# Masked softmax of a matrix product on one core: rows gathered over four batches in 16 KB runs, and the mask read as whole half-blocks

## The chip, the core and the metric

The kernel runs on one core of a Trainium2 chip. The metric is device time in microseconds. The core has a matrix engine (PE, TensorE), a vector engine (DVE), an activation engine (ACT), GpSimd (POOL), a queue engine that issues transfers (SP), and 16 DMA engines that move data between the chip's HBM and the on-chip memory SBUF. Products land in PSUM banks and are read from there by DVE and ACT. A transfer of 128 partitions is cut into one packet for each contiguous run and spread over the 16 DMA engines.

## What is computed

```
y = scale * matmul(x, weight)          # x: 16 x 512 x 512, weight: 512 x 512, scale 0.125
y = where(mask == 1, y, -1e9)          # mask: 1 below the diagonal, 0 on it and above
out = softmax(y, axis=-1)              # float32, 16 x 512 x 512
```

The mask is strictly lower triangular: row r sees the columns below r. Rows 0 to 255 (the upper half, h=0) thus need only the first 256 columns of the product, rows 256 to 511 (the lower half, h=1) all 512. Row 0 sees nothing, so its result is uniform, 1/512.

## The kernel before

The work is cut into 16 units. Unit u takes the half h = u % 2 of two neighbouring batches: 512 rows, put on 128 partitions with four neighbouring rows (8 KB) in each. Each unit is one load of 1 MB (`load`, L80), one tile of four row slots, and one store of 1 MB (`store`, L160). Eight input tiles and eight output tiles exist, so unit u+8 uses the tile of unit u.

A unit goes through these steps, each a function:

- `cast` (L85, DVE): x to bf16, one instruction of 128x2048.
- `transpose` (L94, PE): 16 products with the identity, four row slots by four pieces of the inner dimension, into two PSUM tiles.
- `evict` (L104 on DVE, L105 on ACT): one PSUM tile each to SBUF.
- `multiply`: per row slot four matmuls over the inner dimension (L118) with 256 or 512 columns, one matmul (L127) that adds the band of the mask (identity by `band`, 256 columns), and on ACT the exponential with its row sum (L137).
- `normalise`: a reciprocal (L152) and four scalings (L154) on DVE; in upper units POOL writes 1/512 over row 0 (L156).

The mask enters as an additive band: 0 where the mask is 1 and -512 where it is 0. Only the 128x128 blocks on the diagonal are read (256 KB, L164, runs of 512 B). DVE turns them into `diag_bf`, four matmuls with a 0/1 matrix `spread` (L208) put each row where its unit's layout has it, and eight copies (L215, four on DVE and four on ACT) write them into `band`. The rest of `band` is constant and set by memsets.

The order on every engine is the program's order. The opening issues the loads of x for unit 0, of the mask, of the weight and of units 1 to 7 in one row on SP. PE warms up with 12 products of zeros (L173). After the opening, the loop over u does `transpose(u+1)`, `cast(u+2)`, `evict(u+1)`, `multiply(u)`, `normalise(u-1)`, `store(u-1)`, and the load of unit u+7:

```python
        if u >= 1:
            normalise(u - 1)
            store(u - 1)
            if u - 1 + X_BUFS < U:
                load(u - 1 + X_BUFS)
```

SP therefore issues stores and loads one behind another: a load waits on SP until the store ahead of it may be issued. On DVE, `cast(u+2)` stands before `evict(u+1)`: when x of unit u+2 hasn't landed, the eviction waits behind it.

The softmax here doesn't subtract the row's maximum and nothing guards it: scores larger than these inputs give would overflow.

## Time and profile before

| | before |
|---|---|
| time, median of 8 runs | 90.92 us (90.84 to 91.13) |
| time of the profiled execution | 91.02 us |
| its span, first to last instruction | 89.2 us |
| mean granted PE clock | 0.944 |
| busy: PE, DVE, ACT, POOL | 69.7, 60.5, 55.3, 7.3 us |
| DMA: moved, packets, share of 16 engines' span | 34.87 MB, 5280, 93.6% |
| x of one unit (1 MB), issue to landing, median | 14.6 us |
| store of one unit (1 MB), issue to landing, median | 11.6 us |
| weight (1 MB) and mask (256 KB), issue to landing | 8.5 and 6.6 us |

The time is what the device reports for a run; the span is what the profile sees of one execution, 1.8 us less. Busy shares are averages over the span; which engine is the limit must be read stage by stage. An issue-to-landing time holds the waiting behind transfers issued earlier, so it says how far ahead of the DMA engines the queue is, not how long the transfer itself takes. A packet count rests on the length of contiguous runs: 8 KB for x, the output and the weight, 512 B for the mask, and a few bytes for the count-up at the end of each engine's share of a transfer.

### The profile page before, as it was taken

The page shows a single profiled execution, that of the slowest core. Times are in us where ns is not written, and L with a number is a line of the kernel's source. Part 1 is how long each engine was busy: PE and PEld are TensorE (multiplying, and loading weights), DVE is VectorE, ACT ScalarE, POOL GpSimd, SP SyncE. Part 2 cuts the span into 40 slices and gives each one's busy share as a digit, 9 for nine tenths or more (in the row PEclk, how much of TensorE's full clock was granted, in tenths as well). Part 3 has the DMA queues.
Part 4 walks back from the last instruction along what each step waited for, and adds up shares of the span by engine and source line. Part 5 has one row for each costly group of instructions (what it writes and reads, how often), then busy time and mean ns, then how long its engine had stood idle before and what let it go on. Part 6 is the DMA issues. An engine that isn't in the chain of part 4 may idle for free.

```text
span 89.2 us, 1610 instructions
## 1 busy us (share of the span) xinstructions
PE 69.7 (78%) x584; PEld 48.7 (55%) x592; DVE 60.5 (68%) x123; ACT 55.3 (62%) x154; POOL 7.3 (8%) x20
## 2 busy tenths in 40 slices
PE   4946205999999999999999999999999999900000
PEld 1305005794697589569748956975895595400000
DVE  5876914779299949959994996987494996262000
ACT  5402930668787778778777977877797787630000
POOL 7620000002000200200020020002000201000000
PEclk9999997599999999999999999999999999999555
DMA  0869999999999999999999999999999999999960
GB/s 0 323 216 365 419 422 430 437 415 422 419 430 419 419 433 433 404 419 426 433 415 433 437 404 426 433 430 415 426 422 430 415 433 433 419 422 441 426 294 29
DMA packets 5286, 34.95 MB, mean 392 GB/s; under 512 B 544, under 2 KB 1056, under 8 KB 1056
## 3 DMA queue, kind: packets, MB, share of 16 engines
q1 hardware_dynamic: 5280, 34.87, 93.6%
q8 instruction: 4, 0.07, 0.3%
q14 instruction: 2, 0.02, 0.0%
HBM read 18.09 MB, written 16.78 MB: 391 GB/s over the span
## 4 chain that ended last, share of the span: by engine, by line
PE 71%; DMA 12%; DVE 3%; SPq 2%; issue 1%; ACT 1%; DVEq 0%; ACTq 0%
PE py L118 47%; PE pt L94 16%; DMA xf<-in_x_dram 12%; PE py L127 8%; DVE ot L154 1%; DVE xb L85 1%; SPq L80 1%; ACT ot L137 1%; SPq L164 1%; SPq L165 1%; DVEq L264 0%; DVE rinv L152 0%; ACTq L264 0%
## 5 line engine op out<-in xcount | busy, mean ns | idle before, releaser
L118 PE MATMUL py<-w_bf,xt 128*128 128x256 bf16 (+1 forms) x248 | 49.8, 328 | 0.4
L137 ACT ACTIVATE ot<-py 128x256 f32<-128x256 f32 (+1 forms) x64 | 31.2, 493 | 7.7 <-PE py L127 7.4
L118 PEld LDWEIGHTS <-xt 128*128 128x128 bf16 x256 | 24.8, 100 | 12.2
L105 ACT COPY xt<-pt 128x1024 bf16<-128x1024 bf16 x16 | 16.2, 1012 | 14.9 <-PE pt L94 10.3
L85 DVE CAST xb<-xf 128x2048 bf16<-128x2048 f32 x16 | 19.5, 1222 | 7.7 <-DMA xf<-in_x_dram 7.5
L154 DVE TENSOR_SCALAR ot<-ot,rinv 128x256 f32<-128x256 f32 (+1 forms) x64 | 23.5, 431 | 0.8
L94 PE MATMUL pt<-ident_bf,xb 128*128 128x128 bf16 x256 | 17.8, 225 | 6.6 <-DVE xb L85 6.6
L94 PEld LDWEIGHTS <-xb 128*128 128x128 bf16 x256 | 16.6, 116 | 8.5 <-DVE xb L85 7.6
L127 PE MATMUL py<-band,ident_bf 128*128 128x256 bf16 x64 | 17.6, 275 | 0.0
L104 DVE COPY xt<-pt 128x1024 bf16<-128x1024 bf16 x16 | 11.0, 686 | 6.2 <-PE pt L94 6.2
L137 ACT ACTIVATION_READ_ACCUMULATOR ot<-py 128x1 f32 x64 | 12.8, 200 | 0.0
L156 POOL MEMSET ot<- 2x256 f32 x8 | 3.6, 450 | 66.5 <-DVE ot L154 66.5
L127 PEld LDWEIGHTS <-ident_bf 128*128 128x128 bf16 x64 | 6.3, 99 | 4.2
L173 PE MATMUL py<-zeros 128*128 128x512 bf16 x12 | 4.2, 518 | 1.2 <-DVE zeros L170 1.2
L152 DVE RECIPROCAL rinv<-rsum 128x4 f32<-128x4 f32 x16 | 2.7, 168 | 3.2 <-ACT ot L137 3.2
L179 DVE MEMSET ot<- 128x1024 f32 x4 | 3.6, 912 | 0.6 <-issue 0.6
L173 PEld LDWEIGHTS <-zeros 128*128 128x128 bf16 x12 | 1.4, 124 | 3.5 <-issue 1.9
L186 ACT ACT_TABLE_LOAD x1 | 1.3, 1283 | 0.7 <-PEq L250 0.7
L215 ACT CAST band<-py 64x256 bf16<-64x256 f32 x4 | 1.4, 368 | 0.1
L215 DVE CAST band<-py 64x256 bf16<-64x256 f32 x4 | 1.4, 406 | 0.0
L180 POOL MEMSET ot<- 2x256 f32 x4 | 1.2, 301 | 1.5 <-DVE ot L179 1.4
L208 PE MATMUL py<-diag_bf,spread 128*128 128x512 bf16 x4 | 1.0, 377 | 0.2 <-DVE diag_bf L194 0.2
(14 smaller groups left out, 6.6 us busy)
## 6 DMA issues: line engine op xcount, KB each, us to landing
xf<-in_x_dram SPq DMA_DIRECT2D x16, 1024.0 KB, 14.6
out_dram<-ot SPq DMA_DIRECT2D x16, 1024.0 KB, 11.6
w_f<-in_weight_dram SPq DMA_DIRECT2D x1, 1024.0 KB, 8.5
diag_f<-in_mask_dram SPq DMA_DIRECT2D x1, 256.0 KB, 6.6
```

The source lines that it names most:

```text
L85: seq(nc.vector.tensor_copy(xb, st_x.pop(u)))
L94: nc.tensor.transpose(st_pt[u][kt // 2][:, kt % 2, t], xb[:, t].rearrange("p (k kt) -> p kt k", kt=KT)[:, kt], ident_bf,)
L104: seq(nc.vector.tensor_copy(xt[:, 0:2], pt[0]))
L105: seq(nc.scalar.copy(xt[:, 2:4], pt[1]))
L118: nc.tensor.matmul(py[:, :NC], lhsT=xt[:, kt, t], rhs=w_bf[:, kt, :NC], start=(kt == 0), stop=(kt == KT - 1),)
L127: nc.tensor.matmul(py[:, h * HB : NC], lhsT=ident_bf, rhs=band[:, h, t], start=False, stop=True, skip_group_check=True,)
L137: nc.scalar.activation(out=ot[:, t, :NC], in_=py[:, :NC], func=AF.Exp, bias=0.0, scale=float(scale), accum_out=rsum[:, t : t + 1],)
L154: seq(nc.vector.tensor_scalar_mul(ot[:, t, :NC], ot[:, t, :NC], rinv[:, t : t + 1]))
L156: seq(nc.gpsimd.memset(ot[0:2, 0, :HB], 1.0 / N))
L173: seq(nc.tensor.matmul(idle, lhsT=zeros[:, :P], rhs=zeros, start=True, stop=True))
L179: nc.vector.memset(ots[i][:, :, HB:], 0.0)
L215: seq(copy(band[half, :, t, g * P : (g + 1) * P], src[half, :, g]))
```

## The change

Units stay at 512 rows, but two of them now form a group that is loaded and stored together. A group takes one half h of four neighbouring batches: 32 blocks of eight neighbouring rows from each, so a partition holds eight rows, a run of 16 KB. Unit u is row slots 0 to 3 or 4 to 7 of group u // 2 (`slots`), so the halves come in the order upper, upper, lower, lower. `load` and `store` move 2 MB; only the first group is loaded in two pieces of 1 MB, and the first and the last group are stored in two pieces. There are five input tiles and four output tiles of 2 MB.

The mask: partition q now gets rows 2q and 2q+1 of each half as one run of 3 KB (768 numbers, from which the 256 columns of each row's band are taken), 786 KB in all, in two half-blocks. Two DVE instructions make `band` from it. The placing of rows moves into the product that adds the band: `spread[:, j]`, a 0/1 matrix, stands in the place of the identity as the stationary operand (L127 of before). The four placing products, the eight copies, the memsets of `band` and `diag_bf` go away. The mask lands in the last output tile, which is used late.

The opening loads x of unit 0, the weight, the mask, x of unit 1, and then groups 1 to 4. A second run of 12 products of zeros stands after `transpose(0)`. In the first two turns of the loop `multiply(u)` stands ahead of `transpose(u+1)`. The pools of `xb` and `xt` have two tiles each, where they had three.

```diff
-X_BUFS = 8
-OUT_BUFS = 8
-WARM = 12
+X_BUFS = 5
+OUT_BUFS = 4
...
-    xb_pool = ctx.enter_context(tc.tile_pool(name="xb", bufs=3))
-    xt_pool = ctx.enter_context(tc.tile_pool(name="xt", bufs=3))
+    xb_pool = ctx.enter_context(tc.tile_pool(name="xb", bufs=2))
+    xt_pool = ctx.enter_context(tc.tile_pool(name="xt", bufs=2))
...
-    x_r = x.rearrange("(c e) (h p t) k -> c h p e (t k)", e=2, h=2, t=T)
-    out_r = out.rearrange("(c e) (h p t) n -> c h p e (t n)", e=2, h=2, t=T)
-
-    diag_r = bass.AP(tensor=mask.tensor, offset=mask.offset, ap=[[N, P], [P * N + P, KT], [1, P]])
-
+    x_r = x.rearrange("(c e) (h p t) k -> c h p e (t k)", e=E, h=2, t=S)
+    out_r = out.rearrange("(c e) (h p t) n -> c h p e (t n)", e=E, h=2, t=S)
     ident_bf = const.tile([P, P], BF16, name="ident_bf")
     w_f32 = const.tile([P, KT, N], FP32, name="w_f32")
     w_bf = const.tile([P, KT, N], BF16, name="w_bf")
-    diag_f32 = const.tile([P, KT, P], FP32, name="diag_f32")
-    diag_bf = const.tile([P, KT, P], BF16, name="diag_bf")
-    spread = const.tile([P, T, P], BF16, name="spread")
+    spread = const.tile([P, S // 2, P], BF16, name="spread")
     zeros = const.tile([P, N], BF16, name="zeros")
-    band = const.tile([P, 2, T, HB], BF16, name="band")
-    ots = [const.tile([P, T, N], FP32, name=f"ot{i}") for i in range(OUT_BUFS)]
+    band = const.tile([P, 2, 2, HB], BF16, name="band")
+    ots = [const.tile([P, S, N], FP32, name=f"ot{i}") for i in range(OUT_BUFS)]
...
-    def load(u):
-        xf = x_pool.tile([P, T, K], FP32, name="xf")
-        seq(nc.sync.dma_start(xf.rearrange("p t k -> p (t k)"), x_r[u // 2, u % 2]))
-        st_x[u] = xf
+    def slots(u):
+        return slice(T * (u % 2), T * (u % 2) + T)
+
+    def load(g, part=slice(0, S)):
+        if g not in st_x:
+            st_x[g] = x_pool.tile([P, S, K], FP32, name="xf")
+        run = slice(part.start * K, part.stop * K)
+        seq(nc.sync.dma_start(st_x[g].rearrange("p t k -> p (t k)")[:, run], x_r[g // 2, g % 2][:, :, run]))
 
     def cast(u):
         xb = xb_pool.tile([P, T, K], BF16, name="xb")
-        seq(nc.vector.tensor_copy(xb, st_x.pop(u)))
+        seq(nc.vector.tensor_copy(xb, st_x[u // 2][:, slots(u)]))
...
-        h = u % 2
+        h = u // 2 % 2
         NC = (h + 1) * HB
         xt = st_xt.pop(u)
-        ot = ots[u % OUT_BUFS]
+        ot = ots[u // 2 % OUT_BUFS][:, slots(u)]
...
-                    lhsT=ident_bf,
-                    rhs=band[:, h, t],
+                    lhsT=spread[:, (slots(u).start + t) // 2],
+                    rhs=band[:, h, t % 2],
...
-        if u % 2 == 0:
-            seq(nc.gpsimd.memset(ot[0:2, 0, :HB], 1.0 / N))
-
-    def store(u):
-        ot = ots[u % OUT_BUFS]
-        seq(nc.sync.dma_start(out_r[u // 2, u % 2], ot.rearrange("p t n -> p (t n)")))
-
-
-    load(0)
-    seq(nc.sync.dma_start(diag_f32, diag_r))
+        if u % 4 == 0:
+            seq(nc.gpsimd.memset(ot[0:E, 0, :HB], 1.0 / N))
+
+    def store(g, part=slice(0, S)):
+        ot = ots[g % OUT_BUFS]
+        run = slice(part.start * N, part.stop * N)
+        seq(nc.sync.dma_start(out_r[g // 2, g % 2][:, :, run], ot.rearrange("p t n -> p (t n)")[:, run]))
+
+
+    load(0, slots(0))
     seq(nc.sync.dma_start(w_f32, weight.rearrange("(p kt) n -> p kt n", kt=KT)))
-    for u in range(1, X_BUFS):
-        load(u)
+
+
+    RUN = N + HB
+    mask_f32 = ots[OUT_BUFS - 1].rearrange("p t n -> p (t n)")[:, : 2 * RUN].rearrange(
+        "p (h c) -> p h c", h=2
+    )
+    seq(
+        nc.sync.dma_start(
+            mask_f32,
+            bass.AP(
+                tensor=mask.tensor,
+                offset=mask.offset,
+                ap=[[2 * N, P], [HB * (N + 1), 2], [1, RUN]],
+            ),
+        )
+    )
+    load(0, slots(1))
+    for g in range(1, X_BUFS):
+        load(g)
 
 
     nc.vector.memset(zeros, 0.0)
-    idle = psum_y.tile([P, N], FP32, name="py")
-    for _ in range(WARM):
-        seq(nc.tensor.matmul(idle, lhsT=zeros[:, :P], rhs=zeros, start=True, stop=True))
+
+    def spin(n):
+        idle = psum_y.tile([P, N], FP32, name="py")
+        for _ in range(n):
+            seq(nc.tensor.matmul(idle, lhsT=zeros[:, :P], rhs=zeros, start=True, stop=True))
+
+    spin(12)
 
     make_identity(nc, ident_bf)
-    nc.gpsimd.memset(band[:HP, :, :, P:], MASK_NEG)
-    nc.gpsimd.memset(band[HP:, :, :, :P], 0.0)
     for i in range(0, OUT_BUFS, 2):
         nc.vector.memset(ots[i][:, :, HB:], 0.0)
-        nc.gpsimd.memset(ots[i][0:2, 0, HB:], 1.0 / N)
-
-
-    for g in range(2):
-        for e in range(2):
-            seq(
-                nc.scalar.copy(
-                    spread.rearrange("k t (g p e) -> k t g p e", g=2, e=2)[:, :, g, :, e],
-                    ident_bf.rearrange("k (p t) -> k t p", t=T),
-                )
-            )
+        nc.gpsimd.memset(ots[i][0:E, 0, HB:], 1.0 / N)
+
+
+    for e in range(E):
+        seq(
+            nc.scalar.copy(
+                spread.rearrange("q j (p e) -> q j p e", e=E)[:, :, :, e],
+                ident_bf.rearrange("q (p j) -> q j p", j=S // 2),
+            )
...
     cast(0)
-    seq(
-        nc.vector.tensor_scalar(
-            out=diag_bf,
-            in0=diag_f32,
-            scalar1=-MASK_NEG,
-            scalar2=MASK_NEG,
-            op0=ALU.mult,
-            op1=ALU.add,
-        )
-    )
     transpose(0)
+    spin(12)
     evict(0)
-    for t in range(T):
-        pm = psum_y.tile([P, N], FP32, name="py")
-        seq(
-            nc.tensor.matmul(
-                pm, lhsT=spread[:, t], rhs=diag_bf.rearrange("k b c -> k (b c)"), start=True, stop=True
-            )
-        )
-        for g, copy in enumerate((nc.vector.tensor_copy, nc.scalar.copy)):
-            half = slice(g * HP, (g + 1) * HP)
-            src = pm.rearrange("p (h g c) -> p h g c", h=2, g=2)
-            seq(copy(band[half, :, t, g * P : (g + 1) * P], src[half, :, g]))
     seq(nc.vector.tensor_copy(w_bf[:, 0:2], w_f32[:, 0:2]))
     seq(nc.scalar.copy(w_bf[:, 2:4], w_f32[:, 2:4]))
+    for i in range(2):
+        seq(
+            nc.vector.tensor_scalar(
+                out=band[:, :, i],
+                in0=mask_f32[:, :, i * N : i * N + HB],
+                scalar1=-MASK_NEG,
+                scalar2=MASK_NEG,
+                op0=ALU.mult,
+                op1=ALU.add,
+            )
+        )
     cast(1)
 
+
     for u in range(U + 1):
+        if u < 2:
+            multiply(u)
         if u + 1 < U:
             transpose(u + 1)
         if u + 2 < U:
             cast(u + 2)
         if u + 1 < U:
             evict(u + 1)
-        if u < U:
+        if 2 <= u < U:
             multiply(u)
         if u >= 1:
             normalise(u - 1)
-            store(u - 1)
-            if u - 1 + X_BUFS < U:
-                load(u - 1 + X_BUFS)
+            g, second = divmod(u - 1, 2)
+            if g in (0, G - 1):
+                store(g, slots(u - 1))
+            elif second:
+                store(g)
+            if second and g + X_BUFS < G:
+                load(g + X_BUFS)
```

## The prediction

> **What bounds the kernel now.** I read the page's slices first, then the queue, then the chain of waits, then windows of the DMA's rate, and last the timeline at both ends.
>
> ```profile
> PE   4946205999999999999999999999999999900000
> ...
> DMA  0869999999999999999999999999999999999960
> ...
> DMA packets 5286, 34.95 MB, mean 392 GB/s; under 512 B 544, under 2 KB 1056, under 8 KB 1056
> ...
> q1 hardware_dynamic: 5280, 34.87, 93.6%
> ...
> PE 71%; DMA 12%; DVE 3%; SPq 2%; issue 1%; ACT 1%; DVEq 0%; ACTq 0%
> ```
>
> The chain gives PE 71%, but it follows instructions. The slices show TensorE falling silent after slice 34 while the transfers go on for three more. So I ask how long the DMA engines were ever short of work (columns: stretch, its length, busy of PE, PEld, DVE, ACT, POOL, clock, DMA share, GB/s):
>
> ```profile
> 2.00:5.00 3.00, 3.00 (x11) 1.12 (x9) 2.51 (x4) 0.98 (x5) 1.95 (x5) 1.00 0.85 317
> 5.00:7.50 2.50, 0.61 (x6) 0.24 (x5) 1.66 (x2) 0.00 (x0) 0.30 (x1) 1.00 0.51 164
> 7.50:22.00 14.50, 9.47 (x82) 7.08 (x81) 9.57 (x18) 7.99 (x18) 0.45 (x1) 0.88 1.02 428
> 22.00:57.00 35.00, 34.79 (x319) 25.42 (x321) 28.73 (x60) 27.73 (x79) 1.79 (x4) 1.00 1.01 423
> 57.00:86.00 29.00, 20.98 (x175) 14.51 (x176) 17.02 (x41) 17.32 (x53) 1.35 (x3) 0.94 1.01 426
> 86.00:88.30 2.30, 0.00 (x0) 0.00 (x0) 0.00 (x0) 0.00 (x0) 0.00 (x0) 0.50 0.23 96
> ```
>
> And SP's own waits (in total, times, longest):
>
> ```profile
> SPq L160 <- DVE ot L154: 56.8, 16, 13.2
> SPq L264 <- DMA out_dram<-ot: 6.8, 1, 6.8
> ```
>
> From 7.5 to 86 us the engines are never short of work, at 423 to 428 GB/s. The one weak stretch, 5.0 to 7.5, is the mask in 512 B packets. The last line is decisive: the last store waits 6.8 us though a 1 MB transfer takes 2.45, so it stands behind older ones. The kernel is DMA-bound, and TensorE is not far behind.
>
> The trace's records of single transfers say more. Of the 16 engines' shares of each transfer the first lands: x of unit 0 at 5.44, mask 7.55, weight 10.08, then 31 more MB until 86.18 (2.455 us per MB; 2.485 in the load phase, 2.45 in the pure stores at the end). The last engine lands 0.5 us later at 20 us but 2.06 later at the end (88.24): one engine falls 1.38 behind just when a 16 KB instruction fetch passes at 23.0, others after fetches at 36.9, 51.3 and 64.8. So the slowest engine ends the kernel, 1.0 us before the span does.
>
> **What the Trainium skill says.** "DMA: Bandwidth & Descriptors", section Where 436 GB/s comes from, gives 435 GB/s as the ceiling; this trace's 423 to 428 is within 3% of it. The same page, Why small descriptors are slow (HBM only), says each packet carries a fixed overhead. The trace agrees: packets of 4 B, 512 B and 8 KB take 9, 27 and 309 ns. The last two give 0.0367 ns per byte (436 GB/s over 16 engines) plus 8.2 ns. The same page, Why a DMA increments its semaphore by 16 and not by 1, says that the engine count is the largest number up to 16 that divides both outermost sizes: the new 32 rows by 4 batches against 128 partitions still give 16. "TensorE: Matmul & The Clock Gate", What's actually happening, says that an idle window of about 3.4 us halves the clock. Here PE idles from 9.6 to 14.3 and the clock is 0.50 from 14.3 to 17.8.
>
> **The change part by part.** All sums are for the profiled execution: span 89.2, time 91.02, thus 1.8 around the span; the median is 0.1 below it.
>
> *Packets.* x of groups 1 to 7 (14 MB) and stores of groups 1 to 6 (12 MB) move in 16 KB runs. Per engine that is 56 pairs of 8 KB packets among loads and 48 among stores becoming one packet each. No data packet of 16 KB is in the trace; the line gives 610 ns against 618. Bounds: nothing (the run is split back), and 104 x 8.2 = 0.85 us. Stores already take 2.45 us per MB, 306 ns a packet, so I give their pairs half: 56 x 8.2 + 48 x 4 = 0.65 us gained. Transfers fall from 34 to 21, so 13 completion packets of 9 ns per engine: 0.12.
>
> *Mask.* 512 packets of 512 B cost 7.55 - 5.44 = 2.11 us of the queue, though they are only 32 x 27 ns = 0.86 of work per engine. The new load is three times the bytes (786 KB) in 256 packets of 3 KB. The line gives 16 x 121 ns = 1.94. The old packets came one per 66 ns on an engine, and a 3 KB packet takes longer than that gap, so I expect it full. Bounds 1.9 and 2.5; I take 2.0, a gain of 0.1.
>
> *Sum on the DMA.* 0.65 + 0.12 + 0.1 = 0.87 us earlier, as long as the queue never runs empty.
>
> *Does it?* Loads are issued in one burst as before, with no wait: x0a, weight, mask, x0b, four groups of 2 MB. First landings by addition: weight 7.9, mask 9.9, x0b 12.4, x1 17.3, x2 22.2, x3 27.1, x4 32.0. Then SP's order is S0a, S0b, L5, S1, L6, S2, L7, S3 to S6, S7a, S7b, one behind another. TensorE decides when each store is ready. Rows for that:
>
> ```profile
> 24.01 0.89 PE pt L94 x16
> ...
> 27.09 0.89 PE pt L94 x16
> ...
> 31.87 0.89 PE pt L94 x16
> ```
>
> These are pieces of the chain; from the timeline come
>
> ```profile
> 13.06 1.23 DVE L85 CAST xb<-xf 128x2048 bf16<-128x2048 f32 x1 [1.79 <-DMA xf<-in_x_dram]
> ...
> 14.34 1.90 PE L94 MATMUL pt<-ident_bf,xb 128*128 128x128 bf16 x16 [4.76 <-DVE xb L85]
> ...
> 16.69 0.68 DVE L104 COPY xt<-pt 128x1024 bf16<-128x1024 bf16 x1
> ...
> 79.11 1.68 DVE L154 TENSOR_SCALAR ot<-ot,rinv 128x512 f32<-128x512 f32 x4
> ```
>
> The chain's three give a transposition T = 0.89 and an upper-half multiply of 2.19; the next step gives 3.89 for a lower half. In the new order cast(2) stands before evict(1) on VectorE, and cast(2) waits for the whole 2 MB of x1. With 0.5 us for the slowest engine that is 17.8; cast 1.23, eviction 0.68: multiply(1) starts at 19.85 where before it was 19.95. It ends at 22.04. T(2) and T(3) follow (xb is there), so multiply(2) starts at 23.8. Left are 12 T, 6 upper and 8 lower multiplies: 10.7 + 13.1 + 31.1 = 54.9, so TensorE ends at 78.8 (before: 78.1). Last activation, reciprocal and four scalings took 2.65 before, so S7b is issued at 81.45 (before: 80.8).
>
> The DMA wants S1 at 41.7 (ready near 36), S3 at 61 (ready near 47), S6 at 76 (ready near 70). The slowest engine reaches S7b near 84.6; from issue to first packet the first load took 1.56 (0.74 to 2.30), so S7b must be issued by 83.0. Margin 1.5 us: covered, thinly (less if the path from issue to landing is as long as the first load's, see rival b). If that cover goes, every further microsecond of TensorE is a microsecond of the end.
>
> *Edits that cost nothing.* Buffers of xb and xt fall from three to two. cast(u+2) then waits for T(u), evict(u+1) for multiply(u-1), both an iteration old in PE's order. Behind such a cast on VectorE stand an eviction and a normalisation. Two upper units in a row load VectorE with about 3.45 us each against PE's 3.08, so it slips about 0.4 per unit; the next eviction has 2.19 + 0.89 before it is needed, so this hides. Output tiles: 4 x 2 MB is 8 MB as before, but a tile comes free later: unit 14 writes its tile near 71.8 and the slowest engine has stored S3 by 68. x7 lands at 63.1, T(14) wants it near 67. The four spread products, eight band copies (2.8 us on DVE and ACT) go, two tensor_scalar of 0.43 come, all before x0b lands at 12.4; hidden. The spin of 12 fits between T(0) (end 8.3) and multiply(0), which waits for the band near 10.9. The rank of `spread` instead of the identity costs the same weight load.
>
> Forecast: span 88.3, profiled time 90.15, median 90.05.
>
> **The rivals.** (a) *16 KB runs bring nothing*: packets split or stores gain nothing; then 0.12 + 0.1 remain, 90.7. For it: no such data packet is seen. Against: the fetches are recorded as 16 KB packets. (b) *TensorE ends it, slower*: multiply(1) comes after 4.8 us of idle PE (15.1 to 19.85, waiting for x1). If that idle stretch fills a clock window, PE restarts at half speed as it did at 14.3, for 2.0 to 3.4 us, or up to 4.8 if a partly busy window does not restore the clock; it loses half of that, 1.0 to 2.4 us, and every later unit follows. The first load took 5.2 us from issue to the last engine's landing (0.74 to 5.95); S7b with an empty queue would land at 86.65 plus the delay, against 87.4 in the forecast, so this decides from 0.75 (at the latest 1.5) of delay on, and passes the old time at 1.6 to 2.4. The full 2.4 gives 89.05, span 90.05, median 91.75. Against it: an idle of 4.8 us need not hold a whole window of 3.4, and the upper half of the price needs the slow restoration. (c) *The slowest engine's lag shifts*: 2.06 us is made by instruction fetches, four now; PE's program grows by 16 rows only. Two fetches on one engine would add about 1.4: 91.4; a luckier spread saves 0.5: 89.5.
>
> **How the numbers follow.** Forecast 0.57, (a) 0.15, (b) 0.14, (c) 0.07 up and 0.07 down. Faster by 0.2% (below 90.74; this bound is about what a measurement of this kernel can tell from no change) hold the forecast, the lucky part of (c) and nearly half of (a): 0.70. Within 0.2%: the rest of (a) and the mild part of (b): 0.12. Slower: 0.18. The range reaches down to 89.4 (full packet gain, lucky lag) and up to 91.6 (most of (b)); the likeliest case alone has 89.7 to 90.5.
>
> **What would show it.** Right: 16 KB packets of about 610 ns, mask landing 2.0 us after the weight, DMA share 1.0 from 6 us to the end without a weak stretch, the final wait for the last store well above 3 us, x1's cast near 17.8, last matmul near 79. Wrong: a DMA share under 1 ahead of the last store (b), packets of 8 KB in the groups of 16 KB runs (a), or a last landing more than 2.1 us after the first (c).

## The result and the profile after

The changed kernel takes 91.96 us (median of 11 runs, 91.62 to 92.74) beside 90.96 for the kernel before (31 runs on the same chips): the ratio is 1.0115, with a 95% interval of 1.010 to 1.013. The forecast was 90.05, and the range ended at 91.6. The change costs about 1.0 us where 0.9 was to be gained. Landings and lags below are those of one profiled execution of each kernel; that of the kernel after took 91.65 us, 0.31 less than its median.

| profiled execution | before | after |
|---|---|---|
| time, span | 91.02, 89.2 us | 91.65, 89.9 us |
| mean granted PE clock | 0.944 | 0.937 |
| DMA: moved, packets, share | 34.87 MB, 5280, 93.6% | 35.39 MB, 3152, 94.2% |
| last store, first engine's landing | 86.19 us | 87.92 us |
| last store, last engine's landing | 88.24 us | 88.85 us |
| time less last landing | 2.78 us | 2.80 us |

The page of the kernel after: slices, the queue, and the shares in the chain.

```profile
PE   4987984009999999999999999999999999991000
...
PEclk9999999855699999999999999999999999999955
DMA  1999999999999989998999999999999999999590
...
DMA packets 3159, 35.47 MB, mean 395 GB/s; under 512 B 337, under 2 KB 337, under 8 KB 593
...
q1 hardware_dynamic: 3152, 35.39, 94.2%
...
PE 67%; DMA 17%; DVE 3%; SPq 2%; issue 2%; ACT 1%; DVEq 0%; ACTq 0%
```

The packets are fewer, and the DMA row is full from the second slice; the weak stretch of the old mask is gone. There is a new weak slice near the end (38, with a 5), and a low clock in slices 8 to 11. The windows of the kernel after say more (columns as in the prediction: stretch, length, PE, PEld, DVE, ACT, POOL, clock, DMA share, GB/s):

```profile
5.00:7.50 2.50, 1.63 (x6) 0.44 (x5) 1.65 (x2) 0.00 (x0) 0.30 (x1) 1.00 1.01 419
7.50:22.00 14.50, 8.46 (x72) 5.95 (x72) 6.24 (x8) 5.23 (x13) 0.00 (x0) 0.83 1.00 418
22.00:29.50 7.50, 7.45 (x63) 5.13 (x62) 4.40 (x12) 5.02 (x15) 0.45 (x1) 0.87 1.03 435
29.50:32.50 3.00, 3.00 (x28) 1.93 (x27) 2.96 (x8) 2.47 (x6) 0.00 (x0) 1.00 0.95 336
32.50:57.00 24.50, 24.34 (x233) 18.70 (x235) 21.21 (x46) 19.73 (x61) 0.90 (x2) 1.00 1.01 428
57.00:83.00 26.00, 24.05 (x194) 15.80 (x194) 17.89 (x43) 19.32 (x55) 0.45 (x1) 1.00 1.00 426
83.00:85.00 2.00, 0.00 (x0) 0.00 (x0) 0.85 (x3) 0.00 (x0) 0.00 (x0) 1.00 0.55 229
85.00:88.00 3.00, 0.00 (x0) 0.00 (x0) 0.00 (x0) 0.00 (x0) 0.00 (x0) 0.58 0.88 363
```

Two stretches fall out. From 29.5 to 32.5 the engines are busy at a share of 0.95 and yet move only 336 GB/s, where the kernel before moved 426 in the same stretch: the packets themselves last longer. The queue's records put the long packets at 30.0 to 31.5, among the last of the opening's loads (group 4, called x4 as in the prediction), just ahead of the first store. This change from loads to stores is called the turn below. Between 30 and 32 a 16 KB packet lasts 782 ns on average and 1684 at most, against a median of 611. From 83 to 85 the share is 0.55: some engines had nothing to do. SP's waits in the kernel after (in total, times, longest):

```profile
SPq L163 <- DVE ot L156: 70.1, 10, 21.3
SPq L282 <- DMA out_dram<-ot: 4.4, 2, 2.4
```

The wait at the end is 4.4 us in two parts where it was 6.8 in one: the last store was issued at 83.9, not at 81.45. PE's part of it is in its timeline (start, duration, idle time before it and what ended that):

```profile
14.75 1.08 PE L96 MATMUL pt<-ident_bf,xb 128*128 128x128 bf16 x16 [1.53 <-DVE xb L87]
20.35 1.04 PE L120 MATMUL py<-w_bf,xt 128*128 128x256 bf16 x4 [4.51 <-DVE xt L106]
```

PE idles for 4.51 us before the second unit's multiply and then runs at half clock: four matmuls take 1.04 us. So rival (b), a TensorE that comes too late, is there in the profile. The landings of single engines' shares say that it doesn't set the end. Of the last but one store, the first share landed at 84.04 and the last at 86.42, a lag of 2.38 us. The last share of the last store landed at 88.85, only 2.43 later, which is one share's own time (2.45 per MB): that engine never ran dry. The first engines did: they landed the last store 3.88 us after the one before, at 87.92, still 0.93 ahead of the slowest.

### The profile page after: what moved, and what is told of

Read it like the earlier page. It is cut to its first block, busy times and chain, and to the rows that moved or that the text cites. A ratio compares the mean times of both kernels' runs of the same rounds, so it can differ in the third digit from the quotient of the medians.

```text
span 89.9 us, 1588 instructions
## 1 busy us (share of the span) xinstructions
PE 72.7 (81%) x593; PEld 49.3 (55%) x600; DVE 58.6 (65%) x118; ACT 54.4 (61%) x150; POOL 3.1 (3%) x12
## 3 DMA queue, kind: packets, MB, share of 16 engines
q1 hardware_dynamic: 3152, 35.39, 94.2%
## 4 chain that ended last, share of the span: by engine, by line
PE 67%; DMA 17%; DVE 3%; SPq 2%; issue 2%; ACT 1%; DVEq 0%; ACTq 0%
PE py L120 46%; DMA xf<-in_x_dram 17%; PE pt L96 14%; PE py L129 8%; DVE ot L156 1%; SPq L83 1%; DVE xt L106 1%; ACT ot L139 1%; SPq L167 1%; SPq L175 0%; DVEq L282 0%; DVE rinv L154 0%; ACTq L282 0%; DVE xb L87 0%; DVEq L87 0%
## 5 line engine op out<-in xcount | busy, mean ns | idle before, releaser
L120 PE MATMUL py<-w_bf,xt 128*128 128x256 bf16 (+1 forms) x249 | 50.8, 333 | 4.9 <-DVE xt L106 4.5
L96 PE MATMUL pt<-ident_bf,xb 128*128 128x128 bf16 x256 | 16.8, 219 | 2.4 <-DVE xb L87 2.4
L129 PE MATMUL py<-band,spread 128*128 128x256 bf16 x64 | 17.9, 280 | 0.0
L194 PE MATMUL py<-zeros 128*128 128x512 bf16 x24 | 8.1, 505 | 1.2 <-DVE zeros L189 1.2
L129 PEld LDWEIGHTS <-spread 128*128 128x128 bf16 x64 | 6.4, 100 | 4.3
L194 PEld LDWEIGHTS <-zeros 128*128 128x128 bf16 x24 | 2.8, 122 | 5.1 <-issue 2.7
L158 POOL MEMSET ot<- 4x256 f32 x4 | 1.8, 448 | 64.5 <-DVE ot L156 64.5
L200 DVE MEMSET ot<- 128x2048 f32 x2 | 3.5, 1765 | 0.8 <-issue 0.8
L206 ACT COPY spread<-ident_bf 128x128 bf16<-128x128 bf16 x4 | 1.3, 524 | 0.0
L217 ACT CAST w_bf<-w_f 128x1024 bf16<-128x1024 f32 x1 | 1.0, 1048 | 0.0
```

The source lines that it names most:

```text
L96: nc.tensor.transpose(st_pt[u][kt // 2][:, kt % 2, t], xb[:, t].rearrange("p (k kt) -> p kt k", kt=KT)[:, kt], ident_bf,)
L120: nc.tensor.matmul(py[:, :NC], lhsT=xt[:, kt, t], rhs=w_bf[:, kt, :NC], start=(kt == 0), stop=(kt == KT - 1),)
L129: nc.tensor.matmul(py[:, h * HB : NC], lhsT=spread[:, (slots(u).start + t) // 2], rhs=band[:, h, t % 2], start=False, stop=True, skip_grou ...
L194: seq(nc.tensor.matmul(idle, lhsT=zeros[:, :P], rhs=zeros, start=True, stop=True))
L200: nc.vector.memset(ots[i][:, :, HB:], 0.0)
L206: nc.scalar.copy(spread.rearrange("q j (p e) -> q j p e", e=E)[:, :, :, e], ident_bf.rearrange("q (p j) -> q j p", j=S // 2),)
```

## The experiments

Three theories stood at first. The **TensorE theory**: its late start delays the last store. The **packet theory**: the 16 KB packets, or the transfers of 2 MB, slow the queue. The **spread theory**: the way in which the rows are walked, or the order of the transfers, sets the engines further apart, and the slowest one ends the kernel. In the expectations, T is the TensorE theory, and D says that the slowest DMA engine would end as late anyway; G blames the gathering from four batches, and O the groups of 2 MB, their order or the later first store.

### Making TensorE early, and going back to 8 KB packets

`e1_spin` keeps PE busy in its idle stretch, `e2_evict` lets the eviction of unit 1 pass the cast that waits for x1, `e3_x1half` loads group 1 in two pieces, and `e4_8k` moves every group as two transfers of 1 MB, in packets of 8 KB, still two loads and then two stores. All start from the kernel after:

```diff
 e1_spin, in the loop, behind transpose(u + 1)
+        if u == 0:
+            spin(22)
 e2_evict, in the loop
+        if u == 0:
+            evict(u + 1)
         if u + 2 < U:
             cast(u + 2)
-        if u + 1 < U:
+        if 1 <= u and u + 1 < U:
             evict(u + 1)
 e3_x1half, in the opening
-    for g in range(1, X_BUFS):
+    load(1, slots(0))
+    load(1, slots(1))
+    for g in range(2, X_BUFS):
         load(g)
 e4_8k, wherever a group is moved
-        load(g)
+        load(g, slots(0))
+        load(g, slots(1))
...
-                store(g)
+                store(g, slots(0))
+                store(g, slots(1))
```

> 22 products of zeros stand behind transpose(1), so TensorE doesn't idle while it waits for x of group 1; nothing else changes. Theory T (TensorE finishes too late, and part of that is the half clock after the 4.5 us wait): no half-clock stretch near 17 to 24, the first multiply after the wait takes 2.2 us instead of 3.9, the last matmul ends near 79.6 instead of 81.2, the last store is issued about 1.6 us earlier (near 82.3) and the time falls by 0.5 to 1.5 us to 90.5 to 91.4. Theory D (the slowest DMA engine would end as late anyway): TensorE ends earlier just the same, the last landing stays near 88.8, and the time stays within 0.3 of 91.96 (91.65 in a run like the profiled one).

> In the first turn of the loop evict(1) stands ahead of cast(2) on VectorE, so multiply(1) no longer waits for x of group 1. Theory T: multiply(1) starts near 17 instead of 20.35, multiply(2) near 22 to 23 instead of 26.1, last matmul near 77 to 78, last store issued near 80 to 81, DMA share 1.0 up to the last store, time 90.3 to 91.2. Theory D: the same on TensorE, but the last landing stays near 88.8 and the time is 91.5 to 92.0.

> x of group 1 is loaded in two pieces of 1 MB (8 KB runs) as group 0 is, nothing else changes. Theory T: cast(2) starts near 15.5 instead of 18.5, multiply(1) near 17.5, multiply(2) near 22, last matmul near 77, time 90.3 to 91.2. Theory D: last landing near 88.8, time 91.5 to 92.0.

> Every load and store of a group is two transfers of 1 MB with 8 KB runs at 16 KB pitch; order of work, rows and mask are those of the changed kernel. TensorE starts as early as in the experiment that halves group 1 alone. If the 16 KB runs are worth what the forecast gave them (0.65 us), it is 0.5 to 1 us slower than that experiment. If 16 KB packets make the slowest DMA engine lag more (theory D: 2.4 us here against 2.06 before), the lag of the last landing falls to about 2 us and it is no slower, or faster by up to 0.5.

Measured: `e1_spin` 92.21 us (ratio to before 1.0123, 1.0081 to 1.0165), `e2_evict` 92.0 (1.0121, 1.0084 to 1.0159), `e3_x1half` 91.85 (1.0100, 1.0073 to 1.0127), `e4_8k` 92.29 (1.0142, 1.0124 to 1.016). The first two did to PE what they should. The page's clock and the timeline of `e1_spin`:

```profile
PEclk9999999999999999999999999999999999998555
```

```profile
15.39 4.91 PE L194 MATMUL py<-zeros 128*128 128x512 bf16 x21
20.14 0.60 PE L120 MATMUL py<-w_bf,xt 128*128 128x256 bf16 x4
```

The clock is full until TensorE's work ends, and four matmuls take 0.60 instead of 1.04. In `e2_evict` the multiply of unit 1 starts at 15.98; the timeline and SP's waits there:

```profile
15.98 0.39 PE L120 MATMUL py<-w_bf,xt 128*128 128x256 bf16 x2 [0.34 <-DVE xt L106]
```

```profile
SPq L284 <- DMA out_dram<-ot: 7.3, 2, 4.9
```

The last store was issued near 81.4, with 7.3 us of waiting left after it, and the kernel is no faster for it. The TensorE theory falls: these two runs remove the lateness and keep the whole loss. Where the loss sits then is in the windows of `e2_evict`:

```profile
29.50:32.50 3.00, 2.95 (x32) 2.42 (x32) 3.00 (x6) 2.20 (x5) 0.00 (x0) 1.00 0.95 322
...
87.00:88.00 1.00, 0.00 (x0) 0.00 (x0) 0.00 (x0) 0.00 (x0) 0.00 (x0) 0.50 0.18 74
88.00:89.00 1.00, 0.00 (x0) 0.00 (x0) 0.00 (x0) 0.00 (x0) 0.00 (x0) 0.50 0.06 25
```

and of the kernel before:

```profile
29.50:32.50 3.00, 3.00 (x28) 1.92 (x27) 1.88 (x4) 2.15 (x8) 0.19 (x1) 1.00 1.01 426
...
87.00:88.00 1.00, 0.00 (x0) 0.00 (x0) 0.00 (x0) 0.00 (x0) 0.00 (x0) 0.50 0.16 66
88.00:89.00 1.00, 0.00 (x0) 0.00 (x0) 0.00 (x0) 0.00 (x0) 0.00 (x0) 0.50 0.00 0
```

A share of 0.06 in the stretch from 88 to 89 is one of 16 engines still at work; in the kernel before there is none. The landings agree. The first engine's last landing is 86.31 in `e2_evict` and 86.19 before; the last engine's is 89.27 and 88.24. So of the 1.93 us by which `e2_evict` misses the forecast (92.08 profiled against 90.15), 0.99 are in the first engines (85.32 forecast) and 0.91 in the lag (2.97 instead of 2.06). That lag isn't made at 30 us alone: it is 2.00 at x3 and 2.57 at the first store, but 2.22 again at 57 us, and it rises to 3.00 at x7, the last load, between 62 and 65 us.

The first engines' part (S0a and S0b are the two pieces of the first store): up to x3 they are 0.15 late; x4 takes 5.42 us instead of 4.89, and S0a and S0b another 0.30 beyond their 4.9; from there on 20 MB in 48.44 us, 2.422 per MB, the forecast rate to 0.1 us in all. The gain of the 16 KB packets was there, and the turn at 30 us took it back. In `e4_8k` the same turn costs 0.1 us in the first engines (391 GB/s in that stretch), but the gain isn't there either: they end at 86.51. The packet theory is thus half right: the 16 KB packets have their own price at the turn, but without them the kernel is no faster, and the intervals of the two don't separate.

### The geometry alone, on the kernel before

`f1_four` is the kernel before with its 8 KB runs taken from four batches instead of two; `f2_fourload` does this to the loads only, `f3_fourstore` to the stores only. `f4_two16k` goes the other way: `e2_evict` with 16 KB runs from two batches.

```diff
 f1_four (f2_fourload: the x lines only; f3_fourstore: the out lines only)
-    x_r = x.rearrange("(c e) (h p t) k -> c h p e (t k)", e=2, h=2, t=T)
-    out_r = out.rearrange("(c e) (h p t) n -> c h p e (t n)", e=2, h=2, t=T)
+    x_r = x.rearrange("(c e) (h p t) k -> c h p e (t k)", e=4, h=4, t=T)
+    out_r = out.rearrange("(c e) (h p t) n -> c h p e (t n)", e=4, h=4, t=T)
...
-        seq(nc.sync.dma_start(xf.rearrange("p t k -> p (t k)"), x_r[u // 2, u % 2]))
+        seq(nc.sync.dma_start(xf.rearrange("p t k -> p (t k)"), x_r[u // 4, u % 4 // 2 + 2 * (u % 2)]))
 f4_two16k, on e2_evict (out likewise)
-    x_r = x.rearrange("(c e) (h p t) k -> c h p e (t k)", e=E, h=2, t=S)
+    x_r = x.rearrange("(c e) (p t) k -> c p e (t k)", e=2, t=S)
...
-        seq(nc.sync.dma_start(st_x[g].rearrange("p t k -> p (t k)")[:, run], x_r[g // 2, g % 2][:, :, run]))
+        seq(nc.sync.dma_start(st_x[g].rearrange("p t k -> p (t k)")[:, run], x_r[g][:, :, run]))
```

> The kernel before with one difference: each 1 MB transfer of x and of the output takes 32 runs of 8 KB from each of four batches (a quarter of the rows) instead of 64 from each of two; sizes, count, order and queue stay. The rows then meet the wrong mask rows and the output is permuted; the work is the same. Theory G (four batches at 1 MB pitch make packets slow in the turn from load to store and leave one DMA engine about 3 us behind): slow packets before the first store, last landing 2.8 us or more behind the first, time 91.6 to 92.3. Theory O (the cause lies in the 2 MB groups, their order or the later first store, not in the geometry): same as before, 90.8 to 91.1, lag near 2.0.

> The kernel before with only the loads of x taken from four batches, stores from two as before (rows land in other places of the output, the work is the same). Theory G with the loads as the cause: 91.5 to 92.2; with the stores as the cause, or theory O: 90.8 to 91.1.

> The kernel before with only the stores spread over four batches, loads as before (rows land in other places of the output, the work is the same). Theory G with the stores as the cause: 91.5 to 92.2; with the loads as the cause, or theory O: 90.8 to 91.1.

> The changed kernel with the eviction ahead of the cast in the first turn (so that TensorE is early), and with its groups of 2 MB taken as 64 runs of 16 KB from each of two batches instead of 32 from each of four; sizes, count and order stay (rows then meet the wrong mask rows, the work is the same). Theory G: group 4 lands 4.9 us behind group 3 without slow packets, the lag of the last engine is 2.0 to 2.4, and the time is 90.0 to 90.7, as forecast. Theory O: as with four batches, 91.8 to 92.2.

Measured: `f1_four` 91.79 (1.0083, 1.0059 to 1.0108), `f2_fourload` 91.41 (1.0052, 1.0032 to 1.0071), `f3_fourstore` 90.99 (1.0002, 0.9994 to 1.001), `f4_two16k` 91.96 (1.0110, 1.0083 to 1.0138). Loads from four batches cost 0.43 us of the 90.98 beside them, loads and stores together 0.81, stores alone nothing. `f1_four` moves the same bytes in the same packets as the kernel before; its windows at the end:

```profile
87.00:88.00 1.00, 0.00 (x0) 0.00 (x0) 0.00 (x0) 0.00 (x0) 0.00 (x0) 0.50 0.14 57
88.00:89.00 1.00, 0.00 (x0) 0.00 (x0) 0.00 (x0) 0.00 (x0) 0.00 (x0) 0.50 0.04 16
```

Its first engine is 0.23 earlier than before's (85.96) and its last 0.71 later (88.95): the whole loss is lag, 3.00 us. In `f4_two16k` the lag is 2.80 from only two batches, so the number of batches isn't the only thing that makes it. But the price of the turn is smaller there: with the same 16 KB packets its first engines lose 0.29 us over x4, S0a and S0b (5.13, 2.46 and 2.49), against 0.83 in `e2_evict`. So that price depends on the batches as well as on the size of the packets.

The Trainium skill has one entry near this: "DMA: Bandwidth & Descriptors", section Latency and other measured facts, which reports copies that become up to twice as slow when their rows lie at large powers of two in HBM, and calls the reason, a clash of channels, an inference. Neighbouring batches lie 1 MB apart here. The direction agrees, but in these runs the rate outside the turn doesn't fall; only the spread between engines grows, so that entry doesn't settle it.

### What the slow turn hangs on

`g1_perm` exchanges the data of groups 0 and 4 among the loads, `g2_xbufs4` has four input tiles, so that the first stores come one group earlier, `g4_nope` leaves out TensorE's work and the evictions, all three on `e2_evict`; `g3_xbufs11` gives the kernel before eleven input tiles.

```diff
 g1_perm
-        seq(nc.sync.dma_start(st_x[g].rearrange("p t k -> p (t k)")[:, run], x_r[g // 2, g % 2][:, :, run]))
+        seq(nc.sync.dma_start(st_x[g].rearrange("p t k -> p (t k)")[:, run], x_r[(2, 0, 1, 1, 0, 2, 3, 3)[g], g % 2][:, :, run]))
 g2_xbufs4
-X_BUFS = 5
+X_BUFS = 4
 g3_xbufs11
-X_BUFS = 8
+X_BUFS = 11
 g4_nope: transpose and evict are empty, of multiply the exponential stays
-    xb_pool = ctx.enter_context(tc.tile_pool(name="xb", bufs=2))
+    xb_pool = ctx.enter_context(tc.tile_pool(name="xb", bufs=4))
...
-                    in_=py[:, :NC],
+                    in_=xb[:, t, :NC],
```

> The changed kernel with the early eviction; the loads take their rows in another order of batches (groups 0 and 4 exchanged: group 0 reads batches 8 to 11, group 4 reads batches 0 to 3; both upper halves), the stores as before, so the output is permuted. If the slow packets at 29.5 to 31.5 us belong to the data of group 4 (its place in HBM), they go from there and group 4 lands 4.9 us behind group 3 instead of 5.4. If they belong to the turn from the first long stretch of loads to the first store, they stay at 29.5 to 31.5 and group 4 takes 5.4.

> The changed kernel with the early eviction and four input tiles instead of five, so that the first store stands behind group 3. Turn: the slow packets move to 24.5 to 26.5 us, group 3 takes 5.4 and group 4 4.9. Data of group 4: they stay with group 4. The time stays within 0.4 of 92.0 if the last engine's lag stays at 2.9 to 3.3, and falls to 91 or less if the lag falls to 2.

> The kernel before with eleven input tiles instead of eight: the first store comes after 11 MB of x (near 35 us) instead of 8 MB. If a longer stretch of pure loads makes the first turn slow and pushes the late engine further back, the first store's landing comes 0.5 us or more late and the last landing is 2.5 us or more behind the first, time 91.3 to 92.0. If not: as before, 90.8 to 91.1.

> The changed kernel with the early eviction, without TensorE's transpositions and products, and without the evictions: ACT takes the exponential of the cast x directly. Loads, stores, their sizes and order stay; TensorE's program is only the products of zeros, so its instruction fetches during the run go away. If the fetches put one engine behind and that engine ends the kernel, the last landing is at most 1 us behind the first, the last landing near 87.2, the time near 90.0. If the lag comes from the transfers themselves, it stays at 2 to 3 us and the time at 91.5 to 92.2. The first engine's last landing (86.3) tells the price of the first turn in both cases.

Measured: `g1_perm` 92.03 (one run), `g2_xbufs4` 93.88 (1.0337, 1.0285 to 1.0388), `g3_xbufs11` 90.96 (1.0009, 0.9996 to 1.0023), `g4_nope` 91.33 (its 20 runs lie from 90.43 to 92.07; without the three longest, of which the profiled one, 91.84, is one, the ratio is 1.0026, 1.0005 to 1.0046). One line each of the windows of `g1_perm`, `g2_xbufs4` and `g4_nope`:

```profile
29.50:32.50 3.00, 2.95 (x33) 2.43 (x32) 3.00 (x6) 2.39 (x6) 0.00 (x0) 1.00 1.00 360
```

```profile
24.00:27.00 3.00, 2.87 (x27) 1.77 (x26) 2.48 (x6) 1.87 (x7) 0.00 (x0) 1.00 1.05 393
29.50:32.50 3.00, 2.95 (x32) 2.42 (x32) 3.00 (x6) 2.18 (x6) 0.00 (x0) 1.00 1.06 412
```

```profile
29.50:32.50 3.00, 0.00 (x0) 0.00 (x0) 2.96 (x7) 2.62 (x9) 0.00 (x0) 0.50 0.92 328
```

With other data the long packets stay at 29.5 to 31.5 (360 GB/s, x4 5.32 us); with four tiles they come at 25 to 26 (393), and 30 us is quiet (412). So the slow packets go with the turn from loads to stores, not with an address or a moment. They also come without any TensorE work. The time of `g2_xbufs4` says nothing on this: its queue ran dry between 72 and 76 us, for want of input tiles. A deeper input pool does nothing to the kernel before.

`g4_nope` shows a second thing. Without TensorE's program there are none of its instruction fetches, and the lag is 0.29 us until x3. In the profiled execution it then grows, to 0.85 at 35 us, 1.97 at x6 and 2.69 at the end, so a lag can grow without fetches. But that execution is one of the three longest. In every trace here the time is the last landing plus 2.7 to 2.9 us; by that, the shortest run of 90.43 landed near 87.6, a lag of about 1.3 us if its first engines ended at 86.33 too (an estimate). The median is 0.67 us below that of `e2_evict`, so the fetches, or something else that goes with TensorE's work, may hold a part of the time.

In the other kernels a first fetch of 16 KB sets one engine back by 1.0 to 1.5 us between 19 and 25 us, in the kernel before too; what sorts them comes later.

### The order of loads and stores

`h1_pairs` is the kernel before, the same transfers of 1 MB from two batches, but two stores and then two loads. `h2_altern` is `e4_8k` with store and load in turn. `h3_one` takes each transfer of the kernel before from one batch. `i1_actmask` issues the mask of the kernel before from ACT's queue.

```diff
 h1_pairs
-            store(u - 1)
-            if u - 1 + X_BUFS < U:
-                load(u - 1 + X_BUFS)
+            if u % 2 == 0:
+                store(u - 2)
+                store(u - 1)
+                if u - 1 + X_BUFS < U:
+                    load(u - 2 + X_BUFS)
+                    load(u - 1 + X_BUFS)
 h2_altern, on e4_8k
-            if g in (0, G - 1):
-                store(g, slots(u - 1))
-            elif second:
...
+            store(g, slots(u - 1))
+            if g + X_BUFS < G:
+                load(g + X_BUFS, slots(u - 1))
 h3_one (out likewise)
-    x_r = x.rearrange("(c e) (h p t) k -> c h p e (t k)", e=2, h=2, t=T)
+    x_r = x.rearrange("b (p t) k -> b p (t k)", t=T)
...
-        seq(nc.sync.dma_start(xf.rearrange("p t k -> p (t k)"), x_r[u // 2, u % 2]))
+        seq(nc.sync.dma_start(xf.rearrange("p t k -> p (t k)"), x_r[u]))
 i1_actmask
-    seq(nc.sync.dma_start(diag_f32, diag_r))
+    seq(nc.scalar.dma_start(diag_f32, diag_r))
```

> The kernel before, with stores and loads issued in pairs (two stores of 1 MB, then two loads of 1 MB) instead of in turn; rows, runs of 8 KB from two batches, and results stay. If the grouping to 2 MB makes the turns costly, the landings around the first store come 0.5 us late in all and the last engine is 2.6 us or more behind at the end: 91.4 to 92.2. If only the place of the runs in HBM matters, 90.8 to 91.1 and a lag near 2.0.

> The kernel of the experiment with 8 KB runs throughout (rows over four batches, all transfers 1 MB), with a store and a load in turn, half a group each, as the kernel before has it, instead of two stores and two loads. If the grouping is the cause: lag near 2, 91.0 or less. If the place of the runs is the cause: as the experiment in pairs, 91.9 to 92.4, lag near 3.

> The kernel before with each transfer of 1 MB taken from one batch (128 neighbouring runs of 8 KB) instead of 64 from each of two; sizes, order and queue stay, rows meet the wrong mask rows. If the lag grows with the number of batches that a load is taken from (two: 2.0, four: 2.7 to 3.0), it is at most 2.0 here and the time 90.7 to 91.0. If any other geometry than the tuned one is worse, 91.3 or more.

> The kernel before with one difference: the mask's transfer (256 KB in packets of 512 B) is issued by ACT on its own queue instead of by SP, between x of unit 0 and the weight. If the 2.1 us that it takes from the queue are gaps between its small packets (0.86 us of work per engine), the packets of x and of the weight fill the gaps, every later transfer lands about 1.2 us earlier, and, as the DMA engines end the kernel, the time falls by about 1.2 us to 89.7. If TensorE or the lag of the slowest engine takes its place: 90.3 to 91.0.

Measured: `h1_pairs` 92.58 (1.0184, 1.0155 to 1.0213), `h2_altern` 91.86 (1.0107, 1.0092 to 1.0122), `h3_one` 90.67 (0.998, 0.9972 to 0.9989), `i1_actmask` 91.6 (1.0076, 1.0059 to 1.0092). The windows of `h1_pairs` and, below, of `h3_one`:

```profile
87.00:88.00 1.00, 0.00 (x0) 0.00 (x0) 0.00 (x0) 0.00 (x0) 0.00 (x0) 0.50 0.27 115
88.00:89.00 1.00, 0.00 (x0) 0.00 (x0) 0.00 (x0) 0.00 (x0) 0.00 (x0) 0.50 0.06 25
89.00:90.00 1.00, 0.00 (x0) 0.00 (x0) 0.00 (x0) 0.00 (x0) 0.00 (x0) 0.50 0.02 8
```

```profile
87.00:88.00 1.00, 0.00 (x0) 0.00 (x0) 0.00 (x0) 0.00 (x0) 0.00 (x0) 0.50 0.04 16
88.00:89.00 1.00, 0.00 (x0) 0.00 (x0) 0.00 (x0) 0.00 (x0) 0.00 (x0) 0.50 0.00 0
```

The order alone costs the kernel before 1.74 us (92.58 against 90.84), more than the whole change. In `h1_pairs` the tail of one engine reaches into a third stretch. Its last store also came late, so that the first engines landed it 3.15 us after the one before; but the lag was 3.45 one transfer earlier, and the slowest engine ends at 89.82 from there without a pause. Undoing the grouping in the changed kernel brings back 0.3 us (by the ratios, 1.0142 to 1.0107), to the level of `f1_four`. `h3_one` ends 0.2% earlier, by its first engines (85.63) and not by its lag (2.23); but 0.51 of their 0.56 us is there when the mask lands (7.04 against 7.55), so the trace doesn't show that the single batch made it.

`i1_actmask` was an attempt to save the weak stretch of the old mask. The windows of its opening:

```profile
2.00:5.00 3.00, 3.00 (x8) 1.07 (x7) 2.51 (x4) 1.43 (x5) 1.95 (x5) 1.00 0.60 187
5.00:7.50 2.50, 1.50 (x4) 0.30 (x2) 0.44 (x1) 0.00 (x0) 0.30 (x1) 1.00 1.00 415
```

The first engines were 0.74 us earlier than before's at the last store but one (83.00 against 83.74). But the mask, now first, left the engines 2.2 us apart from the start, the lag there was 3.57, and the kernel is slower. Earlier first engines with a later end: this is the plainest run for the slowest engine as the limit.

### All kernels side by side

Landings are of the last store in the profiled execution, with the lag taken one transfer earlier where the last store came late (marked *). `g2_xbufs4`, whose queue ran dry, is left out. Each row is one execution, and its time differs from the median by up to 0.5 us (those of `e1_spin`, `e3_x1half` and `e4_8k` are the longest of four), so small differences of lag say nothing. The two columns ahead of the end's give the lag of the transfers that first landed near 30 (27 to 30) and near 40 us (37 to 40).

| kernel | lag near 30 | near 40 | at the end | first engine | last engine | median |
|---|---|---|---|---|---|---|
| before | 1.85 | 1.95 | 2.05 | 86.19 | 88.24 | 90.92 |
| after | 2.08 | 2.16 | 2.38* | 87.92 | 88.85 | 91.96 |
| e1_spin | 2.01 | 2.38 | 3.34 | 86.25 | 89.59 | 92.21 |
| e2_evict | 2.00 | 2.11 | 2.97 | 86.31 | 89.27 | 92.0 |
| e3_x1half | 1.93 | 2.25 | 3.36* | 86.35 | 89.54 | 91.85 |
| e4_8k | 2.00 | 2.89 | 3.22 | 86.51 | 89.72 | 92.29 |
| f1_four | 1.88 | 2.87 | 3.00 | 85.96 | 88.95 | 91.79 |
| f2_fourload | 1.99 | 2.09 | 2.66 | 86.09 | 88.75 | 91.41 |
| f3_fourstore | 1.70 | 1.80 | 2.08 | 86.12 | 88.20 | 90.99 |
| f4_two16k | 2.08 | 2.80 | 2.80 | 86.13 | 88.93 | 91.96 |
| g1_perm | 1.65 | 1.81 | 2.85 | 86.34 | 89.19 | 92.03 |
| g3_xbufs11 | 1.97 | 1.93 | 1.99 | 86.10 | 88.09 | 90.96 |
| g4_nope | 0.29 | 0.67 | 2.69 | 86.33 | 89.03 | 91.33 |
| h1_pairs | 2.23 | 3.23 | 3.45* | 87.06 | 89.82 | 92.58 |
| h2_altern | 1.77 | 2.64 | 2.65 | 86.46 | 89.11 | 91.86 |
| h3_one | 2.11 | 2.26 | 2.23 | 85.63 | 87.86 | 90.67 |
| i1_actmask | 3.29 | 3.68 | 3.57* | 86.40 | 89.02 | 91.6 |

The profiled time is the last engine's landing plus 2.74 to 2.89 us in every kernel. The first engines of nearly all runs end between 86.0 and 86.5, so it is the lag that sorts them. Near 30 us the lag is 1.65 to 2.23 everywhere but in the last row and in `g4_nope`: most of that is the first fetch. Later, in some kernels, single packets last far longer than their kind: 8 KB packets by 829 ns in `f1_four` at 36 us, 836 and 953 in `e4_8k` and `h2_altern` at 32, 902 in `h1_pairs` at 37; 16 KB packets by 1073 and 1068 in the kernel after and `e2_evict` at 31. In the kernel before, in `f3_fourstore`, `g3_xbufs11` and `h3_one` none is over by more than 0.55 us once the opening's first transfers are through. In `f2_fourload`, `f4_two16k` and `g4_nope` no single packet is that long, and several of some 0.6 us make the lag.

The records don't name the engine, but a packet starts within 10 ns of the end of the one before it on the same engine. Followed back in this way from the last packet of the kernel after, the slowest engine meets one fetch (at 23.8) and then the packet at 31. In `e2_evict` it meets one fetch (20.6), the packet at 31, and two more that are 0.34 and 0.28 us too long at 62 and 63 us, where its lag jumps by 0.8. In `f4_two16k` it is one fetch and two packets near 32 (0.59 and 0.50). No second fetch stands in these three. With 8 KB packets the steps back aren't unique; there only the lag, which rises at the same time, says that the long packets were the slowest engine's. The jump of 0.8 at x7 is in `e1_spin`, `g1_perm` and `g4_nope` too, the last of them without any fetch of TensorE's.

## Why the prediction was wrong

Its first reading held: the DMA engines bound the kernel, and the slowest of them ends it. Two steps failed, both in what was made of that, and a third error was hidden behind them. The profiled execution missed the forecast by 1.50 us (91.65 against 90.15): its first engines were 1.17 us late at the last store but one, and the lag there was 0.32 larger.

- **"Sum on the DMA: 0.87 us earlier, as long as the queue never runs empty."** The terms were right as sizes: 16 KB packets take 611 ns (610 forecast), 3 KB packets 121 (121), the mask landed 2.17 us after the weight (2.0; bounds 1.9 to 2.5), and outside the turn the first engines ran at the forecast rate. What lacked is a term for the turn from loads to stores, where packets of 16 KB became longer without the queue running empty: 0.86 us of the 1.17 (0.50 at x4, 0.36 at S0a and S0b), and 0.83 in `e2_evict`. Nothing in the profile of before has such a stretch, since its 8 KB loads and stores turn at 426 GB/s.
- **The lag of 2.06 us was carried over unchanged.** It was put down to fetches alone, and since the program hardly grew, a larger one got 0.07 in rival (c). In the kernel before, one fetch does make 1.4 us of it (0.48 to 1.85), but two edits of the change enlarge the lag: loads from four batches (`f2_fourload`, `f1_four`) and stores and loads in pairs (`h1_pairs`, `h2_altern`). The kernel after has 2.38, `e2_evict` 2.97: this term is 0.32 in the one profiled execution and 0.91 in the other. The mechanism that rival (c) named, a second fetch on one engine, isn't on the slowest engine in either trace. Two of the prediction's own signs came: a DMA share under 1 ahead of the last store (b), and a lag of more than 2.1 us (c).
- **Rival (b)** happened, and was hidden. x1's last share landed at 18.34 (17.8), the second multiply began at 20.35 (19.85) after 4.51 us without work, and the clock was 0.50 from 17.2 to 24.0, so the third began at 26.1 (23.8) and the last store was issued at 83.9 (81.45). The prediction had this as a rival, and its forecast had TensorE in time. By its estimate, 86.65 plus the delay of 2.45, the store would land at 89.1; the slowest engine landed it at 88.85, straight behind the store before, so the delay cost nothing. The first engines, which had run dry, landed it at 87.92, later than the 87.4 that the forecast had for the last of all: with the DMA engines as forecast, the delay would have cost about 0.5 us (an estimate from these two landings). `e1_spin`, `e2_evict` and `e3_x1half`, with the last store in time in the first two, are no faster than the kernel after.
- **Rival (a)**, 16 KB runs that bring nothing, is near the truth by its size and not by its reason: the packets weren't split, they gave their gain and lost it at the turn. Against `e4_8k`, the first engines of `e2_evict` are 0.20 us earlier.
- **"Edits that cost nothing"** held: no wait on the smaller pools or the output tiles shows on the path to the end.

Four things stay open. Why a packet at a turn lasts up to 1 us longer, and why the longest of them fell to an engine that was already late, no run shows. How much of the extra lag is the number of batches and how much the order can't be told apart as a sum: `f4_two16k` has the order without the four batches, `f1_four` the four batches without the order, and each makes a lag of about 3; `e4_8k`, which has both, took 92.29, less than `h1_pairs` with the order alone (92.58). How much of the time is the fetches' isn't known: `g4_nope` is without them, but without TensorE's work too. And no run has the gain of the 16 KB packets without the turn and the larger lag, so the forecast's gain was seen in the packets and never in the time.

No version that computes the same result beat the kernel before; `g3_xbufs11` is level with it.

## What to carry to other kernels

In these kernels, bound by their transfers, the end is the landing of the slowest of 16 engines. What the first fetch had put it behind was still there at the end wherever the queue stayed full; where it ran dry, in `g2_xbufs4`, the lag fell from 3.89 to 0.17. So read each transfer's first and last landing, not the mean rate, which was 426 GB/s in kernels 1% apart. The order of loads and stores and the number of places that one transfer reads from act on that spread, by more (0.8 to 1.7 us here) than fewer and larger packets saved (0.2 net, the first engines of `e2_evict` against those of `e4_8k`). Before making transfers larger, see whether they are short of the ceiling at all: the Trainium skill, "DMA: Bandwidth & Descriptors", section Measured (HBM→SBUF, 128 partitions, SWDGE, issued from GpSimd), asks for at least 1 MB per transfer, and a row of 1 MB transfers already ran at 423 to 428 GB/s here.

## What the runs showed of the hardware

- A DMA share of 0.95 can stand beside 322 GB/s: the share counts the time of packets, and at a turn the packets are longer. Share and rate must be read together.
- The same 32 transfers of 1 MB in another order took 1.8% longer (`h1_pairs`).
- The first instruction fetch of 16 KB set one engine back by 1.0 to 1.5 us (lag 0.48 to 1.85 in the kernel before, 0.66 to 2.01 in `e2_evict`); the three later fetches of the kernel before left the lag between 1.84 and 2.08.
- A transfer in small packets that gets ahead of the first large one, from another queue, can leave the engines 2.2 us apart (`i1_actmask`).
